# Feed-forward products as pairs of 64-row matmuls, each half in its own PSUM bank

## The chip, the cores and the metric

One core of a Trainium2 chip runs the whole kernel. The metric is the device time of one execution in microseconds (us). A core has TensorE (PE, matrix products; its weight loads are listed as PEld), VectorE (DVE), ScalarE (ACT), GpSimd (POOL) and SyncE (SP, which here issues the transfers of the weights). The products are summed in PSUM, which has eight banks; one bank holds 512 numbers of 4 bytes in each of 128 partitions.

## The reference

One step of a transformer-like layer for 320 positions: 256 of a new stream and 64 of a running one. The part that the change touches is the last line of `finish`:

```python
    x = x + mix @ w_out
    h = rmsnorm(x, ln_ffn)
    return x + jnp.square(jax.nn.relu(h @ w_up)) @ w_down
```

Here `h` is 320 x 2048, `w_up` is 2048 x 8192 and `w_down` is 8192 x 2048, all in 32-bit floating point. Before it come an RMS norm, an input projection (2048 x 3328), window attention with 16 heads, a gated spatial mixing, and the output projection (2048 x 2048).

## The kernel before

All activations lie transposed: channels on the 128 partitions, the 320 positions (`T`) along the free side. `xT` holds the residual stream as 16 slices of 128 channels. A product with a weight matrix takes 128 input channels (one slice `k`) by 128 output channels (one column tile `g`) as the stationary operand, and streams the 320 positions through it.

For accuracy each 32-bit operand is split in two parts of the short format `F32R`: a high part (a ScalarE copy, line 115) and the rest (a VectorE subtraction, line 116). A product is then three matmuls: weight high by activation high, weight high by activation rest, weight rest by activation high (line 138).

`product` (line 157) computes 256 output channels: it takes a PSUM tile `acc` of two banks, one for each column tile, and calls `products` (line 122). That one goes through the input channels in pieces of four slices. For each piece SP loads 512 KB of weights into `w_raw` (lines 130 and 132), ScalarE and VectorE make `w_hi` and `w_lo` (three buffers each), and TensorE does 4 slices x 2 column tiles x 3 terms = 24 matmuls, 96 for 16 slices. If `ps` is a list of two single banks rather than one tile, the last piece goes through the column tiles one after the other (`tail`, lines 135 and 136), so that the first tile's sum is complete earlier.

PSUM: the pool `ps_acc` has two `acc` tiles (four banks), `ps_sc` has two single banks, used as `q0_ps`, `s_ps`, `g_ps` and `vps` in the attention part and free afterwards (`score_bank`), and `ps_m` has two single banks for small products (`misc`).

The attention scores (line 415) are the place where the kernel uses half of the array's rows: a head has 64 channels, two heads share a 128-partition slice, and for `p` = 0 and 1 a matmul of the lower or the upper 64 partitions writes to `s_ps[0]` or `s_ps[1]`. Line 465 transposes the probabilities on TensorE with all 128 rows. Both are plain 32-bit products.

The feed-forward part (lines 630 to 656) has four blocks of 2048 hidden channels. In each block eight up products (16 slices of `H2H` and `H2L`, the parts of the normalised input) give 256 hidden channels each. Line 639 reads `acc`, applies ReLU and the row norm `r2`, line 641 squares, line 644 makes the high part `FH` and line 645 the rest `FL`. Then eight down products over the block's 16 slices add to `xT` at line 654. The last block's slices of `xT` go out by DMA as they are done; the last product of all takes two `misc` banks (`apart`), and its second column tile is added and sent in two halves.

The engines take their instructions in the order in which the program's scheduler put them; each waits on semaphores for what it needs. The loads of the weights are in one chain on SP (line 109), each as early as a buffer is free.

Of the kernel before, what the change touches and what calls it, by code (L numbers as in the profile page):

```python
# [11 lines left out]
AF = mybir.ActivationFunctionType  # L12
ALU = mybir.AluOpType
AX = mybir.AxisListType

P = 128
T = 320
# [3 lines left out]
KT = DM // P  # L21
DFF = 8192
FB = 16
# [3 lines left out]
HD = 64  # L27
# [3 lines left out]
def hymba_step_kernel(ctx: ExitStack, tc: tile.TileContext, i, o):  # L31
    nc = tc.nc
# [12 lines left out]
    def misc():  # L45
        return ps_m.tile([P, 512], F32, name="misc", tag="misc")

    def score_bank(p, name="s_ps"):
        return ps_sc.tile([P, 512], F32, name=f"{name}{p}", tag=f"s{p}")
# [4 lines left out]
    def blk(name, shape, dt=F32):  # L54
        return actp.tile(shape, dt, name=name, tag="B", bufs=6)
# [3 lines left out]
    xT = const.tile([P, KT, T], F32, name="xT")  # L59
# [23 lines left out]
    for _ in range(4):  # L83
        nc.tensor.matmul(out=warm_ps[:, 0:256], lhsT=nc.const_aps.tensor(0.0, [P, P], F32),  # L84
                         rhs=nc.const_aps.tensor(0.0, [P, 256], F32), start=True, stop=True)
# [19 lines left out]
    def load(out, in_):  # L105


        for o_, i_ in [(out, in_)] + [between.pop(0) for _ in range(min(4, len(between)))]:
            with tc.issue_after(loads[-1].ins) if loads else nullcontext():
                loads.append(nc.sync.dma_start(out=o_, in_=i_))  # L110

    def halves(raw, hi, lo, pinned=False):

        pin = tc.keep_in_program_order if pinned else lambda ins: ins
        return (pin(nc.scalar.activation(out=hi, in_=raw, func=AF.Copy)).ins,  # L115
                pin(nc.vector.tensor_tensor(out=lo, in0=raw, in1=hi.bitcast(F32), op=ALU.subtract)).ins)  # L116

    def w_tiles():
        return (wp.tile([P, 4, 256], F32R, name="w_hi", tag="w_hi", bufs=3),
                wp.tile([P, 4, 256], F32R, name="w_lo", tag="w_lo", bufs=3))  # L120

    def products(w, k0, nk, c0, ps, rh, rl, deep=None, between_pieces={}, halves_behind={}):

        wv = w.rearrange("(kt p) n -> p kt n", p=P)
        behind = carry.pop() if carry else None
        steps.clear()
        for a in range(0, nk, 4):
            raw = (deep or wp).tile([P, 4, 256], F32, name="w_raw", tag="w_raw")  # L130
            hi, lo = w_tiles()
            load(raw, wv[:, k0 + a:k0 + a + 4, c0:c0 + 256])
            with tc.issue_after(halves_behind[a // 4]()) if a // 4 in halves_behind else nullcontext():
                high, low = halves(raw, hi, lo)
            tail = isinstance(ps, list) and a + 4 == nk
            for k, g in [(k, g) for g in range(2) for k in range(4)] if tail else [(k, g) for k in range(4) for g in range(2)]:
                kk = a + k
                for x, (w_, r_) in enumerate(((hi, rh), (hi, rl), (lo, rh))):
                    out = ps[g][:, 0:T] if isinstance(ps, list) else ps[:, g, 0:T]
                    with tc.issue_after(behind) if behind else nullcontext():  # L140
                        mm = nc.tensor.matmul(out=out, lhsT=w_[:, k, g * P:(g + 1) * P], rhs=r_(kk),  # L141
                                              start=(kk == 0 and x == 0), stop=(kk == nk - 1 and x == 2))
            steps.append((high, low, mm.ins))
            if a // 4 in between_pieces:
                with tc.issue_after(mm.ins):
                    between_pieces[a // 4]()
                    behind = narrow[-1]
                if a + 4 == nk:
                    carry.append(behind)
# [4 lines left out]
    def acc_tile():  # L154
        return ps_acc.tile([P, 2, 512], F32, name="acc", tag="acc")

    def product(w, k0, nk, c0, rh, rl, deep=None, apart=False, **kw):
        ps = [misc(), misc()] if apart else acc_tile()
        products(w, k0, nk, c0, ps, rh, rl, deep=deep, **kw)
        return ps  # L160
# [38 lines left out]
    def rstd_b(name):  # L199
        return sm.tile([P, T], F32, name=name, tag="rstd_b", bufs=2)  # L200
# [15 lines left out]
    for a, n in [(a, 1) for a in range(8)] + [(a, 2) for a in range(8, KT, 2)]:  # L216
# [9 lines left out]
        if a > 1:  # L226
            high, low = halves(raw, hi, lo, pinned=True)
        else:
            for j in range(2):
                if a or not j:  # L230
                    load(raw[:, j, 0], wv[:, a, j * 1024:j * 1024 + 256])
                high, low = halves(raw[:, j, 0], hi[:, j, 0], lo[:, j, 0], pinned=True)

        for x, (w_, r_) in enumerate(((hi, xh), (hi, xl), (lo, xh))):
            for j, k, g in [(j, k, g) for j in range(2) for k in range(n) for g in range(2)]:
                ps = q0_ps[g] if j == 0 else kv_ps[:, g]
                mm = nc.tensor.matmul(out=ps[:, 0:T], lhsT=w_[:, j, k, g * P:(g + 1) * P], rhs=r_(a + k),  # L237
                                      start=(a + k == 0 and x == 0), stop=(a + k == KT - 1 and x == 2))
# [96 lines left out]
    def values(*xs):  # L335
        for x, vps in zip(xs, [score_bank(1, "vps"), misc()] if len(xs) == 2 else banks(4)):
            t0 = (0, 64, 128, -64, 192, 256)[x]
            n = min(P, T - t0)
            with tc.issue_after(narrow[-1]):
                mm = nc.tensor.transpose(out=vps[0:n, 0:P], in_=kvx[:, 448 + t0:448 + t0 + n], identity=ident)  # L340
            narrow.append(mm.ins)
            for dst, r in (((v0, slice(0, P)), (w3, slice(HD, P))), ((v64, slice(0, P)),),
                           ((v128, slice(0, P)), (w2, slice(0, HD))), ((w2, slice(HD, P)),),
                           ((w3, slice(0, HD)), (vD, slice(HD, P))), ((w4, slice(0, HD)),))[x]:
                nc.vector.tensor_copy(out=dst[r], in_=vps[r, 0:P].rearrange("k (h d) -> k h d", h=2))
# [3 lines left out]
                    halves_behind={2: lambda: rests[-1]})  # L349
# [15 lines left out]
    def keys():  # L365
        for dst, c in ((kn[:, 0:256], slice(0, 256)), (kn[:, 384:448], slice(256, 320))):
            nc.vector.scalar_tensor_tensor(out=dst, in0=zk[:, c], scalar=g_k, in1=rk[:, c], op0=ALU.mult, op1=ALU.mult)
        for h in range(2):
# [12 lines left out]
                    between_pieces={0: first_norms, 2: keys, 3: lambda: values(2, 3, 4, 5)},  # L381
                    halves_behind={1: lambda: q0_out})
# [67 lines left out]
    def attend(i):  # L450
# [34 lines left out]
        if t is not None:  # L485
            for p in range(2):
# [4 lines left out]
                    between_pieces={1: lambda: (norm_q(2, q2_sq), attend(0)), 3: lambda: attend(1)})  # L491
# [111 lines left out]
    wf = ctx.enter_context(tc.tile_pool(name="wf", bufs=7))  # L603
# [6 lines left out]
    for half, (hi, lo, rm) in enumerate(((AH, AL, rm_a), (SH, SL, rm_s))):  # L610
        for g in range(8):
            ps = product(i["w_out"], 8 * half, 8, g * 256, lambda k: hi[:, k], lambda k: lo[:, k], wf)
            t = sm.tile([P, 2, T], F32, name="to", tag="w2", bufs=4)
# [3 lines left out]
            if half == 0:  # L617
                with tc.issue_after(steps[0][1]):
                    nc.vector.scalar_tensor_tensor(out=SL[:, g], in0=gv[:, g], scalar=g_os[:, g:g + 1],
                                                   in1=SH[:, g].bitcast(F32), op0=ALU.mult, op1=ALU.subtract)  # L620
# [6 lines left out]
    r2 = rstd(acc_x, mean_dm, EPS, rstd_b("r2"))  # L627


    hh_, hl_ = (lambda k: H2H[:, k]), (lambda k: H2L[:, k])  # L630
    yv = o["yT"].rearrange("(kt p) t -> p kt t", p=P)
    nb = DFF // (FB * P)
    for b in range(nb):
        FH = [blk(f"FH{h}", [P, 8, T], F32R) for h in range(2)]
        FL = [blk(f"FL{h}", [P, 8, T], F32R) for h in range(2)]
        for g in range(FB // 2):
            ps = product(i["w_up"], 0, KT, (b * FB + 2 * g) * P, hh_, hl_, wf)
            t = sm.tile([P, 2, T], F32, name="tf", tag="w2", bufs=4)
            nc.vector.scalar_tensor_tensor(out=t, in0=ps[:, :, 0:T], scalar=0.0, in1=r2[:, None, :].to_broadcast([P, 2, T]),  # L639
                                           op0=ALU.max, op1=ALU.mult)  # L640
            nc.scalar.activation(out=t, in_=t, func=AF.Square)
            fs = slice(2 * (g % 4), 2 * (g % 4) + 2)
            fh, fl = FH[g // 4][:, fs], FL[g // 4][:, fs]
            nc.scalar.activation(out=fh, in_=t, func=AF.Copy)
            nc.vector.tensor_tensor(out=fl, in0=t, in1=fh.bitcast(F32), op=ALU.subtract)
        fh_, fl_ = (lambda k: FH[k // 8][:, k % 8]), (lambda k: FL[k // 8][:, k % 8])
        for g in range(8):
            last, end = b == nb - 1, b == nb - 1 and g == 7
            ps = product(i["w_down"], b * FB, FB, g * 256, fh_, fl_, wf, apart=end)
            parts = [(slice(2 * g, 2 * g + 2), slice(0, T), ps[:, :, 0:T])] if not end else \  # L650
                [(2 * g, slice(0, T), ps[0][:, 0:T])] + \
                [(2 * g + 1, c, ps[1][:, c]) for c in (slice(0, T // 2), slice(T // 2, T))]
            for a, c, p in parts:
                nc.vector.tensor_tensor(out=xT[:, a, c], in0=xT[:, a, c], in1=p, op=ALU.add)  # L654
                if last:
                    (nc.scalar if c.start else nc.sync).dma_start(out=yv[:, a, c], in_=xT[:, a, c])
# [66 lines left out]
```

## Time and profile before

| | |
|---|---|
| median of three runs | 1246.7 us (1246.15 to 1247.19) |
| span of the profiled execution | 1245.0 us; no separate total was kept for this execution |
| granted TensorE clock | 1.000 |
| TensorE busy | 1240.9 us, 8560 matmuls and as many weight loads |
| VectorE busy | 656.2 us |
| ScalarE busy | 491.3 us |
| DMA | 187.86 MB, 151 GB/s in the mean |

The span runs from the first to the last instruction of the profiled execution. Matmuls are pipelined: one lasts longer than the distance to the next, so busy time adds up to the whole span, and the pace must be read from the starts. A plain 32-bit matmul is recorded as two instructions (two passes), an `F32R` one as one; the profile calls both f32. In a group's line stand the source line, the engine, the operation, the tiles, the shapes and the count; then busy time, mean ns of one, and the idle time before them.

### The profile page before, as it was taken

To read this page: it belongs to the slowest core of one execution; us is meant where nothing else is said; L and a number is where in the kernel's file an instruction comes from. 1 tells how busy PE (TensorE), PEld (TensorE's weight loads), DVE (VectorE), ACT (ScalarE), POOL (GpSimd) and SP (SyncE) were. 2 spreads that over 40 slices of the span, in tenths; PEclk is the share of its full clock that TensorE was granted. 3 is DMA by queue.
4 is the path that set the end of the run, shared out by engine and by line. 5 is a ranking of instruction groups with operands and counts; after the bars stand their busy time and mean duration, and the time that the engine had idled before them with its cause. 6 is when DMAs were issued, how large, how long until landed. Compare 5 with 4: busy or idle time off the path is not lost.

```text
span 1245.0 us, 20317 instructions
## 1 busy us (share of the span) xinstructions
PE 1240.9 (100%) x8560; PEld 1231.7 (99%) x8560; DVE 656.2 (53%) x787; ACT 491.3 (39%) x651; POOL 97.3 (8%) x89
## 2 busy tenths in 40 slices
PE   9999999999999999999999999999999999999998
PEld 9999999999999999999999999999999999999998
DVE  7777775987864444334454434444443344444343
ACT  7435655424543333333343333333333223433321
POOL 1134462201200000000000000000000000000000
PEclk9999999999999999999999999999999999999999
DMA  9744344544444444444444444445444444545540
GB/s 281 211 140 119 106 118 146 189 146 152 151 148 146 150 151 152 153 148 147 148 150 152 153 153 143 149 149 152 153 153 150 142 149 152 153 152 163 168 164 33
DMA packets 186988, 187.86 MB, mean 151 GB/s; under 512 B 6656, under 2 KB 186432, under 8 KB 186896
## 3 DMA queue, kind: packets, MB, share of 16 engines
q1 hardware_dynamic: 186096, 185.38, 48.0%
q8 instruction: 67, 1.10, 0.4%
q0 software_dynamic: 368, 0.93, 0.2%
q10 hardware_dynamic: 432, 0.24, 0.1%
q14 instruction: 25, 0.20, 0.0%
HBM read 182.98 MB, written 3.32 MB: 150 GB/s over the span
## 4 chain that ended last, share of the span: by engine, by line
PE 100%; DVE 0%; DVEq 0%; issue 0%
PE acc L141 93%; PE q_ps L237 1%; PE acc L237 1%; PE misc L141 1%; PE s_ps L415 1%; PE misc L465 0%; PE misc L472 0%; PE misc L320 0%; PE misc L84 0%; PE misc L538 0%; PE misc L477 0%; PE g_ps L551 0%; PE misc L551 0%; PE misc L186 0%; PE misc L187 0%; PE g_ps L553 0%
## 5 line engine op out<-in xcount | busy, mean ns | idle before, releaser
L116 DVE TENSOR_TENSOR w_lo<-w_raw,w_hi 128x1024 fp32r<-128x1024 f32 x332 | 413.3, 1245 | 430.5 <-ACT w_hi L115 422.0
L115 ACT ACTIVATE w_hi<-w_raw 128x1024 fp32r<-128x1024 f32 x332 | 351.8, 1060 | 697.6 <-PE acc L141 660.3
L141 PE MATMUL acc<-H2H,w_hi 128*128 128x320 f32 x1024 | 316.4, 309 | 0.0
L141 PE MATMUL acc<-H2L,w_hi 128*128 128x320 f32 x1024 | 316.4, 309 | 0.0
L141 PE MATMUL acc<-H2H,w_lo 128*128 128x320 f32 x1024 | 316.4, 309 | 0.0
L141 PE MATMUL acc<-FH,w_hi 128*128 128x320 f32 x992 | 306.5, 309 | 0.0
L141 PE MATMUL acc<-FL,w_hi 128*128 128x320 f32 x992 | 306.5, 309 | 0.0
L141 PE MATMUL acc<-FH,w_lo 128*128 128x320 f32 x992 | 306.5, 309 | 0.0
L141 PEld LDWEIGHTS acc<-H2H,w_lo 128*128 128x128 f32 x1024 | 192.2, 188 | 0.0
L141 PEld LDWEIGHTS acc<-H2H,w_hi 128*128 128x128 f32 x1024 | 192.2, 188 | 0.0
L141 PEld LDWEIGHTS acc<-H2L,w_hi 128*128 128x128 f32 x1024 | 192.2, 188 | 0.0
L141 PEld LDWEIGHTS acc<-FH,w_hi 128*128 128x128 f32 x992 | 186.2, 188 | 0.0
L141 PEld LDWEIGHTS acc<-FL,w_hi 128*128 128x128 f32 x992 | 186.2, 188 | 0.0
L141 PEld LDWEIGHTS acc<-FH,w_lo 128*128 128x128 f32 x992 | 186.2, 188 | 0.0
L141 PE MATMUL acc<-XH,w_hi 128*128 128x320 f32 x352 | 110.8, 315 | 0.0
L141 PE MATMUL acc<-XH,w_lo 128*128 128x320 f32 x352 | 108.8, 309 | 0.0
L141 PE MATMUL acc<-XL,w_hi 128*128 128x320 f32 x352 | 108.7, 309 | 0.0
L141 PEld LDWEIGHTS acc<-XH,w_hi 128*128 128x128 f32 x352 | 66.1, 188 | 2.1 <-issue 1.2
L141 PEld LDWEIGHTS acc<-XL,w_hi 128*128 128x128 f32 x352 | 66.1, 188 | 0.0
L141 PEld LDWEIGHTS acc<-XH,w_lo 128*128 128x128 f32 x352 | 66.1, 188 | 0.0
L639 DVE SCALAR_TENSOR_TENSOR tf<-acc,r 128x640 f32<-128x640 f32 x32 | 26.4, 825 | 41.9 <-PE acc L141 41.8
L654 DVE TENSOR_TENSOR xT<-xT,acc 128x640 f32<-128x640 f32 x31 | 25.5, 821 | 41.8 <-PE acc L141 41.8
(221 smaller groups left out, 1060.5 us busy)
## 6 DMA issues: line engine op xcount, KB each, us to landing
w_raw<-in_w_up SPq DMA_DIRECT2D x128, 512.0 KB
w_raw<-in_w_down SPq DMA_DIRECT2D x128, 512.0 KB
w_raw<-in_w_in SPq DMA_DIRECT2D x44, 512.0 KB
w_raw<-in_w_out SPq DMA_DIRECT2D x32, 512.0 KB
w_first<-in_w_in SPq DMA_DIRECT2D x14, 256.0 KB
out_yT<-xT SPq DMA_DIRECT2D x7, 320.0 KB
xT<-in_xT SPq DMA_DIRECT2D x8, 160.0 KB
xT<-in_xT SPq DMA_DIRECT2D x4, 320.0 KB
```

The lines of the kernel that those rows point to most:

```text
L115: return (pin(nc.scalar.activation(out=hi, in_=raw, func=AF.Copy)).ins, pin(nc.vector.tensor_tensor(out=lo, in0=raw, in1=hi.bitcast(F32), ...
L116: pin(nc.vector.tensor_tensor(out=lo, in0=raw, in1=hi.bitcast(F32), op=ALU.subtract)).ins)
L141: mm = nc.tensor.matmul(out=out, lhsT=w_[:, k, g * P:(g + 1) * P], rhs=r_(kk), start=(kk == 0 and x == 0), stop=(kk == nk - 1 and x == 2))
L237: mm = nc.tensor.matmul(out=ps[:, 0:T], lhsT=w_[:, j, k, g * P:(g + 1) * P], rhs=r_(a + k), start=(a + k == 0 and x == 0), stop=(a + k == ...
L415: mm = nc.tensor.matmul(out=s_ps[p][:, j * nk:(j + 1) * nk], lhsT=qT[hs, blk_, a:a + 2].rearrange("p a t -> p (a t)"), rhs=kz[hs, kv, k0:k ...
L639: nc.vector.scalar_tensor_tensor(out=t, in0=ps[:, :, 0:T], scalar=0.0, in1=r2[:, None, :].to_broadcast([P, 2, T]), op0=ALU.max, op1=ALU.mult)
L654: nc.vector.tensor_tensor(out=xT[:, a, c], in0=xT[:, a, c], in1=p, op=ALU.add)
```

## The change

Every matmul of the feed-forward products becomes two: one with the first 64 rows of the weight tile and of the streamed slice, into the bank that it used before, and one with the last 64 rows, into another bank `lower[g]`. The lower sums of even products go to the two score banks, those of odd products to the two `misc` banks. At the end of an up product ScalarE copies the upper sums to SBUF, VectorE adds the lower sums of the two column tiles to them, and the ReLU with the norm then reads SBUF. At the end of a down product the lower sums are added to `xT` by two more VectorE instructions. The last product uses an `acc` tile as all others do; it is made a list of two only after the product, so the order of its last piece is that of the others. The other products of the kernel are unchanged.

```diff
-    def products(w, k0, nk, c0, ps, rh, rl, deep=None, between_pieces={}, halves_behind={}):
+    def products(w, k0, nk, c0, ps, rh, rl, deep=None, between_pieces={}, halves_behind={}, lower=None):
...
-                    with tc.issue_after(behind) if behind else nullcontext():
-                        mm = nc.tensor.matmul(out=out, lhsT=w_[:, k, g * P:(g + 1) * P], rhs=r_(kk),
-                                              start=(kk == 0 and x == 0), stop=(kk == nk - 1 and x == 2))
+                    rows = [(out, slice(0, P))] if lower is None else [(out, slice(0, HD)), (lower[g][:, 0:T], slice(HD, P))]
+                    for o_, r in rows:
+                        with tc.issue_after(behind) if behind else nullcontext():
+                            mm = nc.tensor.matmul(out=o_, lhsT=w_[r, k, g * P:(g + 1) * P], rhs=r_(kk)[r],
+                                                  start=(kk == 0 and x == 0), stop=(kk == nk - 1 and x == 2))
...
+    def lower(g):
+        return [misc(), misc()] if g % 2 else [score_bank(p, "low") for p in range(2)]
...
-            ps = product(i["w_up"], 0, KT, (b * FB + 2 * g) * P, hh_, hl_, wf)
+            low = lower(g)
+            ps = product(i["w_up"], 0, KT, (b * FB + 2 * g) * P, hh_, hl_, wf, lower=low)
             t = sm.tile([P, 2, T], F32, name="tf", tag="w2", bufs=4)
-            nc.vector.scalar_tensor_tensor(out=t, in0=ps[:, :, 0:T], scalar=0.0, in1=r2[:, None, :].to_broadcast([P, 2, T]),
+            nc.scalar.activation(out=t, in_=ps[:, :, 0:T], func=AF.Copy)
+            for a in range(2):
+                nc.vector.tensor_tensor(out=t[:, a], in0=t[:, a], in1=low[a][:, 0:T], op=ALU.add)
+            nc.vector.scalar_tensor_tensor(out=t, in0=t, scalar=0.0, in1=r2[:, None, :].to_broadcast([P, 2, T]),
                                            op0=ALU.max, op1=ALU.mult)
...
-            ps = product(i["w_down"], b * FB, FB, g * 256, fh_, fl_, wf, apart=end)
+            low = lower(g)
+            ps = product(i["w_down"], b * FB, FB, g * 256, fh_, fl_, wf, lower=low)
+            for a in range(2):
+                nc.vector.tensor_tensor(out=xT[:, 2 * g + a], in0=xT[:, 2 * g + a], in1=low[a][:, 0:T], op=ALU.add)
+            if end:
+                ps = [ps[:, 0], ps[:, 1]]
```

## The prediction

> **What bounds the kernel now.** I read the page first, its busy shares, clock row and chain.
>
> ```profile
> span 1245.0 us, 20317 instructions
> PE 1240.9 (100%) x8560; PEld 1231.7 (99%) x8560; DVE 656.2 (53%) x787; ACT 491.3 (39%) x651; POOL 97.3 (8%) x89
> PEclk9999999999999999999999999999999999999999
> PE 100%; DVE 0%; DVEq 0%; issue 0%
> ```
>
> TensorE is the chain from end to end at full clock; VectorE and ScalarE are idle half the time. A busy PE is not a PE at its peak, so next I took the pace of the matmuls: the chain of waits in order of time (start, length, what), and a window over the same stretch.
>
> ```profile
> 349.97 877.65 PE acc L141 x5984
> 1227.62 14.09 PE misc L141 x96
> ```
> ```profile
> 349.97:1227.62 877.65, 877.65 (x5987) 877.65 (x5986) 387.71 (x354) 309.80 (x314) 0.00 (x0) 1.00 0.48 150
> ```
>
> In the stretch of the feed-forward products 5984 matmuls go through in 877.65 us without a break: 877.65 / 5984 = 0.1467 us each. The stretch at line 141 with 96 matmuls is the last product, 14.09 / 96 = 0.1468. So one product of 96 matmuls takes 14.08 us. The window counts (matmuls, weight loads, then VectorE and ScalarE) give 73 ns per PE instruction. Single instructions show how the 0.1467 is made up.
>
> ```profile
> 600.02 0.31 PE L141 MATMUL acc<-H2H,w_hi 128*128 128x320 f32 x1
> 600.03 0.19 PEld L141 LDWEIGHTS acc<-H2L,w_hi 128*128 128x128 f32 x1
> 600.17 0.31 PE L141 MATMUL acc<-H2L,w_hi 128*128 128x320 f32 x1
> 600.17 0.19 PEld L141 LDWEIGHTS acc<-H2H,w_lo 128*128 128x128 f32 x1
> ```
>
> The next weights start loading as soon as a matmul begins, into the same 128 rows, and the next matmul follows 0.15 us after the last; the 0.31 is pipeline depth, overlapped. What a change to these products is worth is decided by this pace, not by the engines beside it: 1 ns on 6144 of them is 6.1 us, 0.5% of the run.
>
> **The change part by part: the matmuls.** Feed-forward up has 4 blocks x 8 products x 16 slices of 128 rows x 2 column tiles x 3 terms = 3072 matmuls, down the same: 6144, or 6144 x 0.1467 = 901 us. Each becomes two of 64 rows, upper and lower half, into different banks: 6144 more matmuls and 6144 more weight loads. The work of a half is not smaller: it still streams 320 columns for each of 6144 weight tiles of 128 columns. If the halves run side by side, a pair takes what the slower half takes.
>
> No one-pass product (the f32r tiles of line 141) runs in 64 rows in this trace. The nearest are the attention scores, line 415: two 64-row halves into two banks, f32 in two recorded passes each, 4 pairs per call. The first two rows end the window after the first and the second matmul; the third is the whole call, the fourth a full-array f32 stretch just before.
>
> ```profile
> 100.49 0.43 PE L415 MATMUL s_ps<-kzv,qT 64*128 64x192 f32 x1
> 100.49 0.43 PE L415 MATMUL s_ps<-kzv,qT 64*128 64x192 f32 x2
> 100.49 0.92 PE L415 MATMUL s_ps<-kzv,qT 64*128 64x192 f32 x8
> 99.69 0.49 PE L465 MATMUL misc<-ident,s 128*128 128x128 f32 x3
> L465 PE MATMUL misc<-ident,s 128*128 128x128 f32 x48 | 6.9, 272 | 0.0
> L415 PEld LDWEIGHTS s_ps<-kzv,qT x80: 182/186/188, 74.5 to 156.7; 64*128 64x128 f32 x80
> L141 PEld LDWEIGHTS acc<-H2H,w_hi 128*128 128x128 f32 x1024 | 192.2, 188 | 0.0
> ```
>
> The second half starts and ends with the first to within 0.01 us. From the first pair's end to the last's: (0.92 - 0.43) / 3 = 0.163 us per pair of 192 columns. The full array: (0.49 - 0.272) / 2 = 0.109 us for 128 columns, 0.85 ns a column, so 0.163 for 192. A pair of halves costs what one full product would: the halves do overlap, and add nothing I can see. A weight load of 64 rows lasts as long as one of 128, 186 against 188 ns.
>
> For the new pairs the price is thus bounded. Above: the halves in line, or the queue issuing at no better than its 73 ns, 4 x 73 = 0.293 us, +901 us over all pairs. Below: the bare stream. The two f32 prices give a slope of (163 - 109) / 64 = 0.84 ns a column; if one pass costs half, 0.42 x 320 = 0.134, an estimate, and 12 ns of the 0.1467 are a handover between matmuls. Without it: 6144 x 12.3 ns = -76 us. I take 0.1467 per pair, zero: the nearest rows say a pair goes at the pace of one, and each half has as many streams and handovers as the full array had.
>
> The Trainium skill ("TensorE: Matmul & The Clock Gate", Part 3, "What overlaps and what doesn't") says that a weight load overlaps matmuls in flight only where the row group differs. By it the full array pays for its loads and two halves could load behind each other, which speaks for a gain (rival B). The trace disagrees in the "only": in the rows at 600.03 the load runs inside a matmul of the same rows.
>
> **Eviction.** The lower halves have to be added. Nearest rows, groups by form and single instructions:
>
> ```profile
> L639 DVE SCALAR_TENSOR_TENSOR tf<-acc,r 128x640 f32<-128x640 f32 x32 | 26.4, 825 | 41.9 <-PE acc L141 41.8
> L297 ACT ACTIVATE kv<-acc 128x640 f32<-128x640 f32 x1 | 0.7, 684 | 0.0
> L654 DVE TENSOR_TENSOR xT<-xT,misc x3: 314/322/489, 1240.0 to 1242.0; 128x160 f32<-128x160 f32 x2, 128x320 f32<-128x320 f32 x1
> ```
>
> Up: a ScalarE copy of `acc`, as line 297, 0.68 us, two VectorE adds of 128x320 at 0.489, and line 639 on SBUF instead of PSUM, its price kept at 0.83. Down: two adds. Together 32 x 0.68 = 22 us of ScalarE and 64 x 2 x 0.489 = 63 us of VectorE over 901 us. The window has VectorE busy 388 of 878 us and ScalarE 310, so there is room. The cover: banks alternate (two `acc` tiles; low halves in the two score banks for even g, the two misc banks for odd g), so a product's banks are wanted again only after the next product, 14.08 us later. Without that cover each up product would pay 0.68 + 0.98 = 1.66 us, 32 x 1.66 = 53 us.
>
> VectorE and ScalarE are queues in order. Behind the waiting adds stand the w_lo subtractions, behind the copy the w_hi copies. Where one block's up products end it looks like this now:
>
> ```profile
> 453.26 0.83 DVE L639 SCALAR_TENSOR_TENSOR tf<-acc,r 128x640 f32<-128x640 f32 x1 [1.35 <-PE acc L141]
> 454.21 1.23 DVE L116 TENSOR_TENSOR w_lo<-w_raw,w_hi 128x1024 fp32r<-128x1024 f32 x1
> 455.67 0.83 DVE L645 TENSOR_TENSOR FL<-tf,FH 128x640 fp32r<-128x640 f32 x1 [0.24 <-ACT FH L644]
> 457.73 1.22 DVE L116 TENSOR_TENSOR w_lo<-w_raw,w_hi 128x1024 fp32r<-128x1024 f32 x1 [1.23 <-ACT w_hi L115]
> ```
> ```profile
> 454.12 0.74 ACT L641 ACTIVATE tf<-tf 128x640 f32<-128x640 f32 x1
> 454.90 0.74 ACT L644 ACTIVATE FH<-tf 128x640 fp32r<-128x640 f32 x1
> 456.63 1.06 ACT L115 ACTIVATE w_hi<-w_raw 128x1024 fp32r<-128x1024 f32 x1 [1.00 <-PE acc L141]
> ```
>
> The next down product begins at once, but slices 14 and 15 need this FH and FL. A slice is 6 x 0.1467 = 0.88 us, so slice 14 is due 12.3 us on; were whole FH tiles waited for, slice 8, 7.04 us on. FL is done at 456.50, 3.3 us after the eviction began. With 1.66 more, and a w_hi and a w_lo slipped in between (1.06 + 1.23), it takes about 7.2. Slice 14 has 5 us to spare; under the stricter reading 0.2 us is lost at each of 4 blocks, at worst another 1 us each. I take zero, with up to 4 us kept for the range. No load or queue of SP changes.
>
> **The tail.** Before, the last product goes by column tile in its last piece and its first tile is evicted early:
>
> ```profile
> 1239.98 0.49 DVE L654 TENSOR_TENSOR xT<-xT,misc 128x320 f32<-128x320 f32 x1 [6.63 <-PE misc L141]
> 1241.39 0.31 PE L141 MATMUL misc<-FH,w_lo 128*128 128x320 f32 x1
> 1241.74 0.55 DVE L654 TENSOR_TENSOR xT<-xT,misc 128x160 f32<-128x160 f32 x2 [1.27 <-PE misc L141]
> 1242.32 0.35 ACTq L656 DMA_DIRECT2D out_yT<-xT  x1
> ```
>
> The last matmul ends at 1241.70 and the adds 0.59 us later (1242.29). After the change `ps` is no list while the product runs, so the column tiles finish together. The first low add can start three pairs (0.44 us) before the end, ends about 0.09 us after it, and then come the second low add, the full add and the two half-width adds: 0.09 + 0.49 + 0.49 + 0.55 = 1.6 us, +1.0 us. The output of 160 KB that left early now leaves with the last ones.
>
> **Sum.** 0 (pairs) + 0 (eviction, hidden) + 1.0 (tail): 1245.0 + 1.0 = 1246.0 us of span. The three runs have a median of 1246.7 (1246.15 to 1247.19), 1.7 above the span; on that scale it is 1247.7, say 1248. With up to 4 us from block ends and a bare margin for the pace, this case's own range is 1246 to 1254.
>
> **Rivals.** B, the handover is hidden: one half's handover passes while the other streams, and a pair takes 0.134 us. For it: 12 ns above the estimated stream, while the f32 pair at 192 columns is at its bare slope. Against it: a half only continues when its own weights are in place, and needs as many as before. 1248 - 76 = 1172; if half is hidden, 1210.
>
> C, slower: a handover in one half stops both. Place: every pair, from the first up product on. The two follow each other, a pair takes 0.134 + 2 x 0.0123 = 0.159, and 1248 + 76 = 1324. It decides as soon as a stop is not shared. For it: by the estimate above the one-pass stream is twice as dense as the f32 one that the trace shows in halves. Against it: the f32 pairs at 0.163 show no second handover.
>
> D, the change doesn't do what it says: one-pass halves go one after the other, or the queue can't issue four instructions in 0.1467 us (37 ns each). For it: 73 ns is all that a long stretch shows. Against it: the score call gets 8 matmuls and 8 loads through in 0.6 us, but from a filled queue. 1248 + 901 = 2149, less if only issue binds.
>
> The skill ("TensorEngine Tiling (Array Packing)", "Instruction Overhead") puts about 60 cycles on each matmul. Were that paid in line, then by the 2.4 GHz of its TensorE page 6144 x 25 ns = 154 us would be added, an estimate between C and D; the start 0.01 us behind its twin in the score rows speaks against it, on few instructions.
>
> **How the numbers follow.** My forecast has 0.48, B 0.25, C 0.13, D 0.14. The range takes in all but D: B's 1172 and C's 1324, each with 1 ns on the pair (6 us) for the estimated slope beyond, 1165 to 1330. A measurement of this kernel can tell about 0.2%, 2.5 us. Faster by that: B, 0.25 with 0.01 of mine, 0.26. The forecast splits, 0.36 within and 0.11 above if block ends or one nanosecond on the pair show. Slower: 0.11 + 0.13 + 0.14 = 0.38.
>
> **What would show it.** In the profile after: twice the matmuls at line 141's successor in the same stretch, the pair starting together and the next pair 0.1467 us on (right), 0.134 (B), 0.159 (C) or 0.29 (D). Two adds of about 0.49 us and a copy of 0.68 per up product, with PE never idle before a product; a gap in PE at slice 8 or 14 of a block's first down product would show the block ends. After the last matmul 1.6 us of adds rather than 0.59. I am wrong if the pace of a pair differs from 0.1467 by more than half a nanosecond, whichever way.

## The result and the profile after

The changed kernel takes 1249.97 us (median of six runs), the kernel before 1246.58 on the same chip: a ratio of 1.0031, 95% interval 1.002 to 1.0043. It is slower by 3.4 us, 0.3%. Two of the six runs, and three of the eight of the old tail below, had a granted clock of 0.998 and took some 1.5 to 2.5 us longer than the others at 0.999 or 1.000, so that these two intervals are wider than the rest. The profiled execution has a span of 1248.0 us against 1245.0.

The page after: span, busy times, the chain by engine.

```profile
span 1248.0 us, 32704 instructions
PE 1241.5 (99%) x14704; PEld 1231.0 (99%) x14704; DVE 708.1 (57%) x915; ACT 509.3 (41%) x683; POOL 97.2 (8%) x89
PE 98%; DMA 0%; SPq 0%; DVE 0%; ACT 0%; issue 0%; POOLq 0%; POOL 0%; DVEq 0%; ACTq 0%
```

6144 matmuls and as many weight loads more, and PE's busy time is nearly the same. One window over the feed-forward part, first of the kernel after, then of the kernel before (stretch, its length, busy time and count of PE, PEld, DVE, ACT, POOL, granted clock, DMA share, GB/s):

```profile
352.00:1243.36 891.36, 891.36 (x12158) 891.36 (x12155) 439.69 (x477) 329.41 (x347) 0.00 (x0) 1.00 0.48 149
```
```profile
352.00:1241.39 889.39, 889.39 (x6066) 889.39 (x6065) 389.66 (x354) 310.85 (x315) 0.00 (x0) 1.00 0.47 148
```

After: 12158 matmuls are 6079 pairs, 891.36 / 6079 = 0.1466 us a pair. Before: 889.39 / 6066 = 0.1466 us a matmul. From 352 us to the last matmul the pairs keep the pace of the full-array matmuls. VectorE has 50 us more to do there and ScalarE 19, and PE waits for neither: its list of waits after (who waits for what; total, number, longest) has a single one in the feed-forward part, and that is ahead of 352 us.

```profile
PE misc L188 <- ACT n_hl L179: 1.2, 1, 1.2
```

So the loss stands before 352 us or behind the last matmul.

Behind the last matmul, VectorE after (start, length, what, in brackets the idle time before):

```profile
1243.27 0.49 DVE L662 TENSOR_TENSOR xT<-xT,misc 128x320 f32<-128x320 f32 x1 [7.95 <-PE misc L143]
1243.86 0.49 DVE L669 TENSOR_TENSOR xT<-xT,acc 128x320 f32<-128x320 f32 x1
1244.26 0.48 DVE L662 TENSOR_TENSOR xT<-xT,misc 128x320 f32<-128x320 f32 x1
1244.78 0.55 DVE L669 TENSOR_TENSOR xT<-xT,acc 128x160 f32<-128x160 f32 x2
```

The last matmul starts at 1243.36 and lasts 0.31, so it ends at 1243.67; the adds end at 1245.33, 1.66 us later instead of 0.59. That is 1.07 us.

The rest is at the start of the first up product. TensorE's instructions there, after, at the first pair and around the two matmuls of the norm:

```profile
339.53 0.31 PE L143 MATMUL acc<-SH,w_lo 128*128 128x320 f32 x1
339.77 0.41 PE L143 MATMUL acc<-H2H,w_hi 64*128 64x320 f32 x1
340.02 0.30 PE L143 MATMUL acc<-H2L,w_hi 64*128 64x320 f32 x1
...
343.98 0.31 PE L143 MATMUL acc<-H2L,w_hi 64*128 64x320 f32 x1
345.51 0.41 PE L188 MATMUL misc<-n_hl,mean_dm 128*128 128x320 f32 x1 [1.23 <-ACT n_hl L179]
345.86 0.41 PE L143 MATMUL low<-H2L,w_hi 64*128 64x320 f32 x1
345.86 0.41 PE L143 MATMUL acc<-H2H,w_lo 64*128 64x320 f32 x1
346.10 0.30 PE L143 MATMUL low<-H2H,w_lo 64*128 64x320 f32 x1
346.11 0.31 PE L143 MATMUL acc<-H2H,w_hi 64*128 64x320 f32 x1
346.35 0.41 PE L189 MATMUL misc<-n_hl,mean_dm 128*128 128x320 f32 x1
346.69 0.41 PE L143 MATMUL low<-H2H,w_hi 64*128 64x320 f32 x1
346.94 0.30 PE L143 MATMUL low<-H2L,w_hi 64*128 64x320 f32 x1
```

Lines 188 and 189 are the two matmuls that average the squares of the residual for the row norm `r2`; the first needs the high part `n_hl` that ScalarE makes from GpSimd's sum `acc_x`. PE stands still for it. In the scheduler's order this matmul stands behind 57 feed-forward matmuls, in the kernel before as in the changed one. Before, 57 matmuls were 57 x 0.1467 = 8.4 us; now they are 28.5 pairs, 4.2 us. The high part is done at 345.95 before and at 345.46 after:

```profile
345.48 0.47 ACT L177 ACTIVATE n_hl<-acc_x 128x320 fp32r<-128x320 f32 x1 [0.72 <-POOL acc_x L500]
```
```profile
344.99 0.47 ACT L179 ACTIVATE n_hl<-acc_x 128x320 fp32r<-128x320 f32 x1 [1.65 <-POOL acc_x L502]
```

The kernel before, at the same instruction:

```profile
348.34 0.31 PE L141 MATMUL acc<-H2H,w_lo 128*128 128x320 f32 x1
348.49 0.31 PE L186 MATMUL misc<-n_hl,mean_dm 128*128 128x320 f32 x1
```

There it follows its predecessor by 0.15 us, 2.5 us after `n_hl` was done. And in the changed kernel each change between 64-row and 128-row matmuls delays two starts. At the first pair the distances are 0.24 and 0.25 us where 0.15 was the pace. The norm's two matmuls stand apart, so there are four more changes; a norm matmul alone between pairs has the late starts of two changes behind each other: 0.24 to line 189, then 0.34, of which 0.10 belongs to the change into full rows and 0.09 to the one back, then 0.25.

As 57 is odd, the norm's matmul parts the two halves of a matmul: behind it the lower half of one starts beside the upper half of the next, at 345.86 and from there on. The pace is the same, so two halves that run side by side need not be of one matmul. But the half at 343.98 and the very last one, at 1243.36, run alone, which makes one step of 0.147 us more.

### The profile page after: what moved, and what is told of

Read it like the earlier page. It is cut to its first block, busy times and chain, and to the rows that moved or that the text cites. A ratio compares the mean times of both kernels' runs of the same rounds, so it can differ in the third digit from the quotient of the medians.

```text
span 1248.0 us, 32704 instructions
## 1 busy us (share of the span) xinstructions
PE 1241.5 (99%) x14704; PEld 1231.0 (99%) x14704; DVE 708.1 (57%) x915; ACT 509.3 (41%) x683; POOL 97.2 (8%) x89
## 4 chain that ended last, share of the span: by engine, by line
PE 98%; DMA 0%; SPq 0%; DVE 0%; ACT 0%; issue 0%; POOLq 0%; POOL 0%; DVEq 0%; ACTq 0%
PE misc L143 35%; PE low L143 35%; PE acc L143 23%; PE q_ps L239 1%; PE acc L239 1%; PE s_ps L417 1%; PE misc L467 0%; DMA w_first<-in_w_in 0%; SPq L110 0%; PE misc L474 0%; PE misc L322 0%; PE misc L540 0%; PE misc L479 0%; PE g_ps L553 0%; PE misc L553 0%
## 5 line engine op out<-in xcount | busy, mean ns | idle before, releaser
L143 PE MATMUL acc<-H2H,w_hi 64*128 64x320 f32 x1024 | 313.5, 306 | 0.0
L143 PE MATMUL acc<-H2H,w_lo 64*128 64x320 f32 x1024 | 313.4, 306 | 0.0
L143 PE MATMUL acc<-H2L,w_hi 64*128 64x320 f32 x1024 | 313.4, 306 | 0.0
L143 PE MATMUL acc<-FH,w_hi 64*128 64x320 f32 x1024 | 313.3, 306 | 0.0
L143 PE MATMUL acc<-FL,w_hi 64*128 64x320 f32 x1024 | 313.3, 306 | 0.0
L143 PE MATMUL acc<-FH,w_lo 64*128 64x320 f32 x1024 | 313.3, 306 | 0.0
L143 PEld LDWEIGHTS acc<-H2H,w_hi 64*128 64x128 f32 x1024 | 188.4, 184 | 0.2 <-issue 0.2
L143 PEld LDWEIGHTS acc<-H2L,w_hi 64*128 64x128 f32 x1024 | 188.4, 184 | 0.0
L143 PEld LDWEIGHTS acc<-H2H,w_lo 64*128 64x128 f32 x1024 | 188.4, 184 | 0.0
L143 PEld LDWEIGHTS acc<-FH,w_hi 64*128 64x128 f32 x1024 | 188.4, 184 | 0.0
```

The lines of the kernel that those rows point to most:

```text
L143: mm = nc.tensor.matmul(out=o_, lhsT=w_[r, k, g * P:(g + 1) * P], rhs=r_(kk)[r], start=(kk == 0 and x == 0), stop=(kk == nk - 1 and x == 2))
```

## The experiments

All edits are to the changed kernel unless the kernel before is named. The first four were timed together against the kernel before (1246.37 us in those runs).

**The norm's matmuls later.** Both are put behind the second piece of weights of the first up product.

```diff
-    r2 = rstd(acc_x, mean_dm, EPS, rstd_b("r2"))
+    acc_hl = two_parts(acc_x)
+    r2 = rstd_b("r2")
...
-            ps = product(i["w_up"], 0, KT, (b * FB + 2 * g) * P, hh_, hl_, wf, lower=low)
+            ps = product(i["w_up"], 0, KT, (b * FB + 2 * g) * P, hh_, hl_, wf, lower=low,
+                         between_pieces={1: lambda: rstd(acc_hl, mean_dm, EPS, r2)} if b == 0 and g == 0 else {})
```

> The changed kernel, with the two row-norm products (mean_dm) of the first up product put behind its second piece of weights, so 48 pairs in instead of 28 and then 31, both together. Theory (pairs are free; about 2.1 us of the 3.4 lost stand at this one place: 1.4 us of waiting for acc_x and some 0.7 us of changing between 128-row and 64-row matmuls twice): the wait goes and one of the two round trips, -1.7 us against the changed kernel, so about 1.0013 of the kernel before (1248.2). Rival (the loss is spread over the pairs or comes from the added eviction): no gain, 1.003 as it was.

Measured: 1248.22 us, a ratio of 1.0015 (1.0006 to 1.0024). It is 1.85 us over the kernel before in the same runs, where the changed kernel was 3.4 over its own, so about 1.5 us are gone (1.8 by the profiles, see below); 1.7 was expected. TensorE at the new place:

```profile
346.89 0.31 PE L143 MATMUL low<-H2H,w_lo 64*128 64x320 f32 x1
347.12 0.41 PE L188 MATMUL misc<-n_hl,mean_dm 128*128 128x320 f32 x1
347.38 0.31 PE L189 MATMUL misc<-n_hl,mean_dm 128*128 128x320 f32 x1
347.61 0.41 PE L143 MATMUL acc<-H2H,w_hi 64*128 64x320 f32 x1
347.62 0.41 PE L143 MATMUL low<-H2H,w_hi 64*128 64x320 f32 x1
347.87 0.31 PE L143 MATMUL acc<-H2L,w_hi 64*128 64x320 f32 x1
```

The wait is gone. What is left of the place are two changes of form in place of four, each with two slow steps: 0.23 to 0.26 us in place of 0.147.

**The old tail.** The last product of all goes back to full rows, two `misc` banks and the order by column tile.

```diff
-            low = lower(g)
-            ps = product(i["w_down"], b * FB, FB, g * 256, fh_, fl_, wf, lower=low)
-            for a in range(2):
+            low = None if end else lower(g)
+            ps = product(i["w_down"], b * FB, FB, g * 256, fh_, fl_, wf, lower=low, apart=end)
+            for a in range(0 if end else 2):
...
-            if end:
-                ps = [ps[:, 0], ps[:, 1]]
```

> The changed kernel, with the last product of all as it was before: 128 rows, two misc banks, one column tile after the other, no lower halves and no extra adds for it. Theory: the adds behind the last matmul go back from 1.6 to 0.6 us, -1.1 us against the changed kernel, 1.0019 of the kernel before. Rival (the end is set by the outputs' transfers, not by the adds): no gain.

Measured: 1249.13 us, 1.0025 (1.0015 to 1.0036), 2.8 us over the kernel before, so about 0.6 us are gone; 1.1 was expected, which left out that the new change of form ahead of the last product takes 0.2. By itself this difference is within the intervals; the next run has the same edit, and there the profile shows it.

**Both.**

> Both edits together. Theory: what is left are the changes of row mode at the start and at the norm, 0.3 to 0.6 us: 1246.9 to 1247.2, 1.0004 of the kernel before, the same within 0.2%. Rival (each pair costs half a nanosecond more, 3 us): 1.002 to 1.003 is left whatever is done at the two places.

Measured: 1247.37 us, 1.0009 (1.0000 to 1.0018). VectorE behind the last matmul is back at what it was:

```profile
1242.66 0.55 DVE L669 TENSOR_TENSOR xT<-xT,misc 128x160 f32<-128x160 f32 x2 [1.27 <-PE misc L143]
```

Of 3.4 us, 2.4 are gone with two edits at two places, while 12096 of the 64-row matmuls are still there. The rival of half a nanosecond per pair would have left 3 us. It falls. The 1.0 us that stays is somewhat over the 0.3 to 0.6 expected: there are four changes of form (first pair, to the norm, back, to the last product), and the next but one experiment prices them at 0.2 us each, 0.8 together. The profiles bear this out: from the last full-row matmul ahead of the first pair to the start of the last matmul of all it is 901.41 us before, 903.83 after, 902.00 with the late norm alone (three changes) and 902.20 with both edits (four). The last two are 0.59 and 0.79 us more than before, 0.2 for each change.

**The eviction alone**, on the kernel before:

```diff
-            nc.vector.scalar_tensor_tensor(out=t, in0=ps[:, :, 0:T], scalar=0.0, ...
+            nc.scalar.activation(out=t, in_=ps[:, :, 0:T], func=AF.Copy)
+            for a in range(2):
+                nc.vector.tensor_tensor(out=t[:, a], in0=t[:, a], in1=ps[:, a, 0:T], op=ALU.add)
+            nc.vector.scalar_tensor_tensor(out=t, in0=t, scalar=0.0, ...
...
+            for a in range(0 if end else 2):
+                nc.vector.tensor_tensor(out=xT[:, 2 * g + a], in0=xT[:, 2 * g + a], in1=ps[:, a, 0:T], op=ALU.add)
```

> The kernel before, full-array products, with the added eviction alone: the ScalarE copy, two VectorE adds and the ReLU from SBUF at each up product, two more VectorE adds at each down product but the last. The adds read acc a second time in place of the lower banks, so the hidden and the output values are other ones; the work is the same. Theory (hidden): 1.000 of the kernel before, within 0.5 us. Rival (the added eviction delays PE at product or block ends): 1.002 to 1.003.

Measured: 1246.51 us, 1.0001 (0.9992 to 1.0010). The copies and adds cost nothing that shows.

Each of the next kernels was timed once, beside one run of the kernel before (1246.34 us, the last one 1246.89).

**Changes of form in number.** Pairs on even slices, full rows on odd ones.

```diff
-                    rows = [(out, slice(0, P))] if lower is None else [(out, slice(0, HD)), ...
+                    rows = [(out, slice(0, P))] if lower is None or kk % 2 else [(out, slice(0, HD)), ...
...
-                                                  start=(kk == 0 and x == 0), stop=(kk == nk - 1 and x == 2))
+                                                  start=(kk == 0 and x == 0), stop=(kk == nk - (1 if r.start == 0 else 2) and x == 2))
```

> The changed kernel with pairs on the even slices and full-array matmuls on the odd ones: 16 changes of row mode per product, 64 products, 1024 in all. Theory (a change costs about 0.1 us into 64 rows at the first pair and 0.2 us around the norm products, because the array must run empty): +0.1 to +0.2 us each, +100 to +200 us, 1350 to 1450. Rival (what was seen there was only the wait): below 1255.

Measured: 1446.58 us, 200.2 us more than the kernel before. The profile has 1028 changes, 16 in each of 64 products and four around the norm: 0.195 us each, if all of the difference is put down to them. TensorE around two of them:

```profile
700.90 0.31 PE L143 MATMUL low<-H2H,w_lo 64*128 64x320 f32 x1
701.14 0.41 PE L143 MATMUL acc<-H2H,w_hi 128*128 128x320 f32 x1
701.38 0.31 PE L143 MATMUL acc<-H2L,w_hi 128*128 128x320 f32 x1
701.53 0.31 PE L143 MATMUL acc<-H2H,w_lo 128*128 128x320 f32 x1
...
701.97 0.31 PE L143 MATMUL acc<-H2H,w_lo 128*128 128x320 f32 x1
702.21 0.41 PE L143 MATMUL acc<-H2H,w_hi 64*128 64x320 f32 x1
702.22 0.41 PE L143 MATMUL misc<-H2H,w_hi 64*128 64x320 f32 x1
702.47 0.30 PE L143 MATMUL acc<-H2L,w_hi 64*128 64x320 f32 x1
```

In either direction the first matmul of the new form comes 0.24 us after its predecessor and the second 0.24 or 0.25 after that, then the pace is 0.147 again: 0.09 + 0.10 = 0.19 us lost per change. Both ways of counting agree. The Trainium skill ("TensorEngine Tiling (Array Packing)", "Key Properties") says that changing the tiling mode drains TensorE. The trace agrees in that the matmuls of the new form start late, and the first lasts 0.41 us in place of 0.31; by the recorded ends, which are modelled, it starts 0.07 us before the last one of the old form is done (701.14 against 701.21).

**One half alone.** The lower halves and their adds are left out.

```diff
-                    rows = ... [(out, slice(0, HD)), (lower[g][:, 0:T], slice(HD, P))]
+                    rows = ... [(out, slice(0, HD))]
...
```

> The changed kernel without the lower halves: 6144 matmuls of the first 64 rows alone in the feed-forward products, no lower banks and none of their adds; half of each sum is left out. Theory (a half streams and hands over at the pace of the full array, 0.1467 us, and its twin costs nothing): pace 0.1467 still, total within 2 us of the changed kernel. Rival (the handover of 12 ns depends on the rows, or two halves get in each other's way): a lone half goes at less than 0.1467, at 0.134 the total would be 1172.

Measured: 1247.76 us. The window over the feed-forward part:

```profile
352.00:1241.00 889.00, 889.00 (x6064) 889.00 (x6063) 383.46 (x354) 324.48 (x347) 0.00 (x0) 1.00 0.46 148
```

889.00 / 6064 = 0.1466 us. A matmul over half the rows takes what one over all of them takes, and its twin in the other half is free. Here the 57 matmuls ahead of the norm's again go one after the other, and the wait is not there.

**Both on the same rows.** The second matmul of a pair takes the first 64 rows too, its bank stays.

```diff
-(lower[g][:, 0:T], slice(HD, P))]
+(lower[g][:, 0:T], slice(0, HD))]
```

> The changed kernel with both matmuls of a pair on the first 64 rows, into the two banks as before; the lower half of each sum is replaced by the upper one again. Theory (the overlap comes from the two halves being different rows): the two go in line, 2 x 0.1467 per pair, 1248 + 901 = about 2150 us. Rival (the overlap comes from the two banks or from the queue): still 0.1467 per pair, about 1250.

Measured: 2148.65 us. Its window:

```profile
352.00:2142.00 1790.00, 1790.00 (x12207) 1790.00 (x12206) 442.61 (x480) 332.95 (x348) 0.00 (x0) 1.00 0.24 74
```

1790 / 12207 = 0.1466 us for each matmul, 0.293 for a pair. The overlap comes from the rows being different; two banks alone do nothing. And the norm's matmul, again behind 57, now starts 8.55 us after the first of them and has no idle time before it:

```profile
347.81 0.41 PE L188 MATMUL misc<-n_hl,mean_dm 128*128 128x320 f32 x1
```

So the wait after comes from the 57 passing in half the time, as these two runs and the late norm show.

**What the 0.1467 us are made of.** Matmuls of 512 columns, on the kernel before. For the last slice of each tile the 512 columns have to start 192 earlier, so that slice enters the sums with other positions; the expectation overlooks this, and the time isn't touched by it.

```diff
-                    out = ps[g][:, 0:T] if isinstance(ps, list) else ps[:, g, 0:T]
+                    n = 512 if WIDE else T
+                    out = ps[g][:, 0:n] if isinstance(ps, list) else ps[:, g, 0:n]
...
+    def wide(tile, k, n):
+        flat = tile.rearrange("p k t -> p (k t)")
+        c = min(k * T, n * T - 512)
+        return flat[:, c:c + 512]
...
+    hh_, hl_ = (lambda k: wide(H2H, k, KT)), (lambda k: wide(H2L, k, KT))
...
```

> The kernel before, with the matmuls of the feed-forward products streaming 512 columns in place of 320; the 192 more are the next columns of the same tile and are not read afterwards, so the result is the same. Theory (a fixed handover of 12 to 13 ns and 0.42 ns a column): 0.227 to 0.228 us a matmul, 6144 x 0.0805 = +495 us, about 1741. Rival (the one-pass stream itself is slower in proportion, 0.1467/320 = 0.458 ns a column): 0.2347 us, +541 us, about 1787.

Measured: 1738.18 us. The longest piece of its chain of waits in order of time:

```profile
350.64 1360.71 PE acc L142 x6003
```

1360.71 / 6003 = 0.2267 us. From 320 to 512 columns the matmul grows by 0.0800 us, 0.417 ns a column; 320 columns are 0.1333 and 13.3 ns are left. Two lengths give a line but don't test it; what speaks for a fixed step is that the slope is the 0.42 that was estimated from the score rows, and that growth in proportion, 0.2347 us, is ruled out. The Trainium skill ("TensorE: Matmul & The Clock Gate", "Wait — 56ns, not 53.3ns?") has N / 2.4 GHz and about 2.5 ns for a warm matmul: the trace agrees with the slope, 0.417 ns, but not with the fixed part, which is 13.3 ns for these matmuls.

**Is the handover the weight load?** Weight tiles of 64 columns in slices 1 to 14, on the kernel before.

```diff
+                    c = HD if NARROW and 0 < kk < nk - 1 else P
...
-                        mm = nc.tensor.matmul(out=out, lhsT=w_[:, k, g * P:(g + 1) * P], rhs=r_(kk),
+                        mm = nc.tensor.matmul(out=out[0:c], lhsT=w_[:, k, g * P:g * P + c], rhs=r_(kk),
```

> The kernel before, full rows, but in slices 1 to 14 of each feed-forward product the weight tile has 64 of its 128 columns, so only 64 output channels of each column tile are summed there; the rest of those sums is left out. Theory (the handover of 13 ns is a fixed step between two one-pass matmuls that change weights): still 0.1467 us a matmul, plus 130 changes of tile form at most, 0 to 25 us on the total, 1246 to 1272. Rival (the handover is the part of the weight load that isn't hidden, so it goes with the columns): 0.140 us a matmul in those slices, 5376 x 6.7 ns = -36 us, 1211 to 1236.

Measured: 1246.88 us, the kernel before 1246.89 beside it. The loads are shorter, in groups by form (the 135 and the 188 are the mean ns of one):

```profile
L142 PEld LDWEIGHTS acc<-H2H,w_lo 128*64 128x64 f32 x896 | 121.2, 135 | 10.2
L142 PEld LDWEIGHTS acc<-XL,w_hi 128*128 128x128 f32 x352 | 66.2, 188 | 0.0
```
```profile
349.66 878.07 PE acc L142 x5984
```

135 ns against 188, and the chain's piece still 878.07 / 5984 = 0.1467 us. The handover goes neither with the rows (one half alone) nor with the columns of the weights. Of the 25 us that were allowed for changes of tile form 0.4 show at most (878.07 against 877.65 in the kernel before). Not every step to 64 columns is like that. In the kernel before, line 472 has weight tiles of 64 columns and sends its outputs to partitions 0 to 63 and 64 to 127 in turn:

```profile
109.03 0.27 PE L465 MATMUL misc<-ident,s 128*128 128x128 f32 x1
109.23 0.32 PE L472 MATMUL misc<-pt,kzv 128*64 128x128 f32 x1
```

It starts 0.20 us after its predecessor, where 0.11 is the pace at line 465; line 465 is a transpose, and which part of the step is the reason no run tests. So the run shows that columns can be left unused; that a change to two halves of columns is free it doesn't show. What the 13.3 ns are, these runs don't settle.

## Why the prediction was right or wrong

**The pairs: right.** The price of zero per pair, taken from the score rows, holds to less than half a nanosecond. Rival B fell: a half does not hand over more cheaply (one half alone), and a pair is no faster than a full matmul. Rival C fell: two handovers are not paid one after the other. The halves start within 0.01 us of each other, so their handovers fall together; whether a stop in one half alone would stop the other, no run shows. Rival D's price was right for what it describes, 2149 against 2148.65 with both matmuls on the same rows, but the halves don't go in line, and the queue does issue four instructions in 0.147 us, for 891 us on end. The estimate of 0.42 ns a column and 12 ns beside it was 0.417 and 13.3; that an F32R pass takes half of a recorded 32-bit one for each column was assumed there, and no row showed it before the run with 512 columns.

**The eviction: right.** Hidden, by the run of its own. VectorE's share grew by 50 us and it had the room. At the block ends I kept up to 4 us; none shows. TensorE, ScalarE and VectorE after, at the first block's end:

```profile
454.88 0.31 PE L143 MATMUL misc<-H2H,w_lo 64*128 64x320 f32 x1
454.89 0.31 PE L143 MATMUL acc<-FH,w_hi 64*128 64x320 f32 x1
```
```profile
456.05 0.69 ACT L646 ACTIVATE tf<-acc 128x640 f32<-128x640 f32 x1
```
```profile
457.31 0.88 DVE L648 TENSOR_TENSOR tf<-tf,misc 128x320 f32<-128x320 f32 x2
460.63 0.83 DVE L655 TENSOR_TENSOR FL<-tf,FH 128x640 fp32r<-128x640 f32 x1 [1.58 <-ACT FH L654]
```

The down product starts at 454.89, and `FL` is done at 461.46, 6.6 us later: within the 7.04 of the stricter reading, with half a microsecond to spare. The forecast of 7.2 was a little high.

**The tail: right.** +1.0 predicted, 1.07 measured, by the four adds named, though the second low add comes after the first full one.

**The sum: 1248 forecast, 1249.97 measured.** The range of 1165 to 1330 had room for rivals B and C, so that the time lies in it says little; the pace of the pairs says more. Of the change itself, 3.4 us, I had 1.0 (and 0.3 of rounding), and I held a change within 0.2%, 2.5 us, for more likely than a larger loss in my own case. The step that failed is the zero between the terms: I priced the pairs, the eviction and the tail, and did not look for other instructions in TensorE's own queue among the pairs. Two things were there. First, changes of form: five of them (first pair, and twice to the norm and back) at 0.195 us are 1.0 us; the trace of before had their price at each score call, in rows I did not read for it. One such call, and beside it a full-row 32-bit matmul (a transpose) behind a full-row `F32R` one:

```profile
82.14 0.31 PE L141 MATMUL acc<-XH,w_lo 128*128 128x320 f32 x1
82.38 0.37 PE L415 MATMUL s_ps<-kzv,qT 64*128 64x128 f32 x1
```
```profile
90.01 0.31 PE L141 MATMUL acc<-XH,w_lo 128*128 128x320 f32 x1
90.16 0.27 PE L465 MATMUL misc<-ident,s 128*128 128x128 f32 x1
```

The first 64-row matmul starts 0.24 us after a full-row one, not 0.15, and the second pair of rows speaks against the step to plain 32-bit numbers as the reason. Second, an order: the norm's matmul stays behind 57 matmuls, and these now pass in half the time. PE then stands from its last matmul's slot to 345.51, 1.54 us where 0.147 is the pace; 0.09 of it is counted to the change of form, 1.30 us to the wait. With the step of the parted halves and the tail: 1.0 + 1.3 + 0.15 + 1.1 = 3.5 us. The medians differ by 3.4, the profiles by 903.83 - 901.41 = 2.4 us up to the start of the last matmul and 1.07 behind it. (The two profiled spans differ by 3.1 only: in the execution after, the products ahead of the feed-forward part ended 0.46 us sooner, the last one starting at 339.53 against 339.98.)

I named the gap in PE that would show the block ends, and looked for waits behind the adds on VectorE; the wait came from the other direction, with TensorE too early. That 57 matmuls stand ahead of the norm's is in the order of both kernels. It is no fixed count: in the run with 512 columns, where each matmul is longer, 43 stand ahead. What the scheduler reckons with for a half matmul is not settled here.

## What to carry to other kernels

Splitting the rows of a product that fills them all gained nothing here: each half still streams every column and hands over as often, and the pair ends when one full matmul would. A lone half took as long as a pair, so half-row matmuls should pay where the contraction is short, as in this kernel's scores, if the two are on different rows and kept together: every change between 64-row and 128-row matmuls cost about 0.2 us, so a stray matmul of the other form belongs next to its like. And when instructions double without the time doubling, look at what else stands among them in the same queue, and when its inputs come.

## What the hardware showed that I had not expected

A change of row form costs 0.195 us in either direction, spread over the first two matmuls. Half the columns of the weights, by contrast, could be left unused from one matmul to the next for at most 0.4 us in 130 changes. The two halves of the rows run side by side even when they belong to different matmuls, or to different products. And the pace of a one-pass matmul of 320 columns, with its 13.3 ns beside the stream, stays at 0.1467 us with 128 or 64 rows and with 128 or 64 columns of weights.
